# Gates' products where rounds of the recurrence meet, the start's transposes behind its products, a seventh place for the experts' weights

## The chip, the core and the metric

One NeuronCore of a Trainium2 chip runs the whole layer. Its engines work side by side, each through its own list of instructions: TensorE (PE, with its weight loads PEld), VectorE (DVE), ScalarE (ACT), GpSimd (POOL), and SyncE (SP), which issues the transfers between device memory and the core's memory. The metric is the time of one execution in microseconds on the device. Of TensorE the profile also shows the clock that was granted, as a share of 2.4 GHz.

## The reference, cut to what matters

```python
mod_x = silu(c) @ ada_w + ada_b               # 2048 -> 6 x 2048, for the tokens and the context
hx = rmsnorm(x) * (1 + sc1) + sh1             # hc likewise; 256 tokens each
px, pc = hx @ w_in, hc @ w_in                 # 2048 columns in; RWKV, attention, 4096 gate columns
yc_r, s_f, s_b = rwkv_branch(shift(pc), 0, 0)       # 16 heads of 64, forward and backward scan
yx_r, _, _     = rwkv_branch(shift(px), s_f, s_b)   # S = S*w - (S kk)(kk a)^T + v k^T ; y = S r
yx_d = diff_out(diff_attn_latent(q, k_all, v_all))
mix = (sigmoid(g0) * (yx_r @ w_pa) + sigmoid(g1) * (yx_d @ w_pb)) @ w_out
x = x + gt1 * mix
h2 = rmsnorm(x) * (1 + sc2) + sh2
x = x + gt2 * moe(h2)     # 32 experts 2048 -> 512 -> 2048, top 2 of one of 4 groups
# an expert: (silu(h w1) * (h w3)) w2
```

All in float32, 256 tokens and 256 of context.

## The kernel before, in words

The program goes in stages. `startup` loads the tokens and the context (`xt`) and scales their rows; `ada_first` multiplies the conditioning vectors by the first columns of ada_w, in four quarters (512 columns of the shift, 512 of the scale and so on), each from eight tiles of weights of 512 KB. A tile comes either from the `raw` places of the start (RAW0, L37, five of them) or from a piece of `xt`, once `tokens` (transposes, L693) has turned `xt` into columns and put its eight pieces on the list `free`. `modulate` (L704 to L724) then applies scale and shift and splits the result into a high and a low half for the products.

Behind the start runs one long background stream: the products of w_in, of ada's rest and of the gates, one tile of 256 KB after another. Each tile of weights is split in two: `whi` by ScalarE (L966), `wlo` by VectorE (L967), or by GpSimd while `self.low` says so. Each tile gives twelve products of 256 columns into `acc` (L490).

In the foreground stands the RWKV recurrence in four rounds, q = 0 to 3, four heads each. A round first computes features (`feats`: decay, `kq` L1091, the bonus `bon` and its product `pcf` L1104), then `within` and `braid` (products inside a chunk, `pa`), then `deltas`. That begins with the substitution `inverse`: 31 steps of a triangular inverse on VectorE (L1428, L1430), a transpose `ZT` (L1433), and TensorE's products `ph` (L1448) and `pz` (L1461). The rest of `deltas` is products (pW, pu, pS, py), with the features of the next round between them. Where a round's last products and the next round's features stand side by side, the rounds meet; the first meeting is that of q = 0 and q = 1. A generator of the foreground yields numbers; they are credits in microseconds, times 0.444, for which the background stream's steps are called in between. `inverse` yields 0.25 + 0.002 n n per step and `deltas` passes it on (times 1.0 for q < 3). That is the order of the program text; the scheduler of the framework then lists each engine's instructions by its own priorities and may move background work up.

The last stage is the experts, 16 pairs. A pair has 12 chunks of weights of 2 MB (four of w1, four of w3, four of w2), loaded by `weights` (L1755) from SyncE. The first eight go to eight places (`first`: four of tag w, xr, xd, ohl, and acc's); all later ones turn round over six (`slots`: w four times, xr, xd). A load waits for the last product that reads what its place held. A pair on TensorE: the products `pa` with w1 and w3 (L1834), the transposes of the gates and of the hidden rows (L1775, L1787), the `gather` of the next pair's tokens (L1766, four groups, each followed by VectorE's sum L1768), the products `po` with w2 (L1868; `down`), and their spread back to tokens (L1885; `back`, added on VectorE L1889, L1892), always one block behind. TensorE's order in this stage is the order of the program text. The last pair adds into `xr` and stores. Behind it stands the largest count of tokens of an expert (`most`, L1917 to L1922), loaded into a register: over 64, a second path would redo the experts, which is not taken here.

Of the kernel before, what the change touches and what calls it, by code (L numbers as in the profile page):

```python
# [10 lines left out]
F32R = mybir.dt.float32r  # L11
# [7 lines left out]
P = 128  # L19
D = 2048  # L20
KT = 16
# [15 lines left out]
RAW0, LOOK0 = 5, 8  # L37
# [140 lines left out]
def host_inputs(a):  # L178
# [10 lines left out]
    h["exp_w2"] = np.ascontiguousarray(np.asarray(a["exp_w2"])[0].reshape(E // 2, 2, 4, P, 4, 512).transpose(0, 4, 3, 1, 2, 5))  # L189
    h["ws"] = pack_parts(a)  # L190
# [6 lines left out]
def f32(ap):  # L197
    return ap.bitcast(F32)


class Body:
# [437 lines left out]
    def ada_first(self, c, w):  # L639
# [3 lines left out]
        for s in range(2):  # L643
            bank = []

            def fn(raw, k0, s=s, bank=bank):
                if k0 == 0:
                    bank.append(self.ps.tile([P, 512], F32, tag="ps", name="ada")[:, 0:w])
                for k in range(k0, k0 + n):
                    j = slice(k % 4 * 32, k % 4 * 32 + 32)  # L650
                    self.nc.tensor.matmul(bank[0][j, :], self.cs[:, k, :], raw[:, k - k0, :], start=(k < 4), stop=(k >= KT - 4),  # L651
                                          tile_position=(0, j.start))
                yield 0.5
                if k0 + n == KT:
                    if s == 0 and c == 0:
                        self.tokens()
                    self.modulate(c // P, w // P, s, bank[0])
# [29 lines left out]
    def tokens(self):  # L687

        nc = self.nc
        for k in range(KT):  # L690
            pt = self.psa.tile([P, 512], F32, tag="acc", name="pt")
            for i in range(4):
                nc.tensor.transpose(pt[:, i * P:(i + 1) * P], self.xt[:, i, k * P:(k + 1) * P], self.ident)  # L693
# [500 lines left out]
    def deltas(self, st, q):  # L1194
# [166 lines left out]
        yield 0.0  # L1361
# [343 lines left out]
    def moe(self, es):  # L1705
# [15 lines left out]
        slots = ["w"] * WB + ["xr", "xd"]  # L1721
        first = slots + ["ohl", wx]
# [24 lines left out]
        def weights(src, e=None):  # L1747
# [11 lines left out]
            return c  # L1759

# [57 lines left out]
        held = []  # L1818
        for pi in range(E // 2):
# [5 lines left out]
            for nm in ("exp_w1", "exp_w3"):  # L1825
# [13 lines left out]
                if last and nm == "exp_w1":  # L1839
                    gt2 = gate2()  # L1840
# [18 lines left out]
            oh, ol = ohl[:, 0], ohl[:, 1]  # L1859

            def down(w, hs, n):

                wd = hs.stop - hs.start
                o = pst("o", 4)[:, 0:wd]
                for f in range(4):
                    for e in range(2):
                        es_ = slice(e * 64, e * 64 + 64)
                        nc.tensor.matmul(o[es_, :], hT[:, f, es_], w[:, e, f, hs], start=(f == 0), stop=(f == 3),  # L1868
                                         tile_position=(0, e * 64))
                if last:  # L1870
                    g = tl("t", [P, 512], 2, tag="hm")[:, 0:wd]
                    nc.vector.scalar_tensor_tensor(g, o, gc, gt2[:, n * 512 + hs.start:n * 512 + hs.stop], ALU.mult, ALU.mult)
                    self.split(g, oh[:, n, hs], ol[:, n, hs])
                else:
                    nc.scalar.activation(oh[:, n, hs], o, AF.Copy, scale=gc)  # L1875
                    nc.vector.scalar_tensor_tensor(ol[:, n, hs], o, gc, f32(oh[:, n, hs]), ALU.mult, ALU.subtract)
                return oh[:, n, hs], ol[:, n, hs], slice(n * 512 + hs.start, n * 512 + hs.stop)
# [37 lines left out]
        pc = pst("t")  # L1915
        for i in range(2):
            nc.tensor.matmul(pc[:, 0:E], K["ones"], S0[:, i, :], start=(i == 0), stop=(i == 1))  # L1917
        most = tl("most", [P, 1])
        nc.vector.tensor_reduce(most, pc[:, 0:E], AX.X, ALU.max)
        mosti = tl("mosti", [P, 1], dt=I32)  # L1920
        nc.vector.tensor_copy(mosti, most)
# [66 lines left out]
```

## Time and profile before

| what | value |
| --- | --- |
| time, median of 3 runs | 2439.36 us (2437.42 to 2444.34) |
| profiled execution, its own time | 2450.88 us |
| its span | 2449.2 us |
| TensorE busy | 2297.4 us, 94% |
| VectorE busy | 1216.8 us, 50% |
| ScalarE busy | 779.1 us, 32% |
| GpSimd busy | 197.1 us, 8% |
| moved by the transfers | 691.46 MB, mean 282 GB/s |

The busy share is a mean over the stages above: the start up to about 60 us, the mixers up to about 1450, the experts from about 1500 on. A matmul row's time is from the start of the first to the end of the last of a run of like instructions, and float32 products appear as two records each. Busy TensorE is not TensorE at its peak, and whether a wait matters depends on the stage.

### The profile page before, as it was taken

The page shows a single profiled execution, that of the slowest core. Times are in us where ns is not written, and L with a number is a line of the kernel's source. Part 1 is how long each engine was busy: PE and PEld are TensorE (multiplying, and loading weights), DVE is VectorE, ACT ScalarE, POOL GpSimd, SP SyncE. Part 2 cuts the span into 40 slices and gives each one's busy share as a digit, 9 for nine tenths or more (in the row PEclk, how much of TensorE's full clock was granted, in tenths as well). Part 3 has the DMA queues.
Part 4 walks back from the last instruction along what each step waited for, and adds up shares of the span by engine and source line. Part 5 has one row for each costly group of instructions (what it writes and reads, how often), then busy time and mean ns, then how long its engine had stood idle before and what let it go on. Part 6 is the DMA issues. An engine that isn't in the chain of part 4 may idle for free.

```text
span 2449.2 us, 45035 instructions
## 1 busy us (share of the span) xinstructions
PE 2297.4 (94%) x18411; PEld 1612.3 (66%) x18411; DVE 1216.8 (50%) x2268; ACT 779.1 (32%) x1455; POOL 197.1 (8%) x260
## 2 busy tenths in 40 slices
PE   6999989899999999999998998999999999999997
PEld 2789977788998787787898985444433433433342
DVE  3355677868658577586865664222222222222223
ACT  3322336555436565566643441000000000000000
POOL 0110011202114233100000000000000000000000
PEclk9999999999999899899999999999999999999999
DMA  8977864657674243363447886899999999999997
GB/s 337 340 241 228 259 218 133 186 174 229 225 228 141 75 123 118 107 190 99 157 156 239 287 314 253 351 428 427 427 428 426 428 428 428 428 427 427 428 427 327
DMA packets 205476, 691.46 MB, mean 282 GB/s; under 512 B 31768, under 2 KB 69328, under 8 KB 179792
## 3 DMA queue, kind: packets, MB, share of 16 engines
q1 hardware_dynamic: 205264, 688.53, 75.2%
q8 instruction: 146, 2.39, 0.4%
q14 instruction: 66, 0.54, 0.1%
HBM read 666.66 MB, written 21.78 MB: 281 GB/s over the span
## 4 chain that ended last, share of the span: by engine, by line
PE 64%; DMA 18%; DVE 9%; issue 4%; ACT 3%; POOL 1%; SPq 0%; DVEq 0%; ACTq 0%; POOLq 0%
PE acc L490 13%; DMA xd<-in_exp_w_dram 10%; PE pa L1834 9%; PE po L1868 9%; PE acc L521 7%; PE pt L1766 5%; PE acc L815 4%; PE pt L1885 3%; DMA raw<-in_ws_dram 2%; DMA w<-in_exp_w_dram 2%; DVE prod L1428 2%; PE pc L1129 1%; PE ada L651 1%; DVE z L1430 1%; DMA g<-gate 1%
## 5 line engine op out<-in xcount | busy, mean ns | idle before, releaser
L966 ACT CAST whi<-raw 128x512 fp32r<-128x512 f32 (+1 forms) x463 | 280.4, 615 | 334.5 <-PE acc L490 150.7
L967 DVE TENSOR_TENSOR wlo<-raw,whi 128x512 fp32r<-128x512 f32 (+1 forms) x415 | 282.4, 693 | 82.6 <-ACT whi L966 80.6
L490 PE MATMUL acc<-xd,whi 128*128 128x256 f32 (+1 forms) x1248 | 267.1, 291 | 1.2 <-ACT whi L966 0.8
L490 PE MATMUL acc<-xr,whi 128*128 128x256 f32 (+1 forms) x1248 | 264.7, 290 | 1.3 <-ACT whi L966 0.8
L1834 PE MATMUL pa<-w,hg 128*64 128x512 f32 x1024 | 226.6, 594 | 15.8 <-DMA w<-in_exp_w_dram 12.5
L1868 PE MATMUL po<-w,hT 128*64 128x512 f32 (+1 forms) x1040 | 230.8, 590 | 1.6 <-DMA w<-in_exp_w_dram 0.8
L490 PEld LDWEIGHTS acc<-xd,whi 128*128 128x128 f32 (+1 forms) x1248 | 205.9, 191 | 19.6 <-issue 14.5
L490 PEld LDWEIGHTS acc<-xr,whi 128*128 128x128 f32 (+1 forms) x1248 | 205.5, 191 | 17.2 <-issue 12.8
L1781 DVE TENSOR_TENSOR hm<-hm,pa 128x512 f32<-128x512 f32 x16 | 11.0, 688 | 405.8 <-PE pa L1834 405.8
L490 PE MATMUL acc<-xr,wlo 128*128 128x256 f32 (+1 forms) x624 | 181.3, 291 | 4.2 <-DVE wlo L967 3.4
L490 PE MATMUL acc<-xd,wlo 128*128 128x256 f32 (+1 forms) x624 | 180.8, 290 | 2.6 <-DVE wlo L967 2.1
L1834 PEld LDWEIGHTS pa<-w,hg 128*64 128x64 f32 x1024 | 71.7, 137 | 165.5 <-issue 132.8
L607 DVE SCALAR_TENSOR_TENSOR ada<-raw,cs,ada 128x512 f32<-128x512 f32 x180 | 135.0, 758 | 90.4 <-DMA raw<-in_ws_dram 90.0
L1868 PEld LDWEIGHTS po<-w,hT 128*64 128x64 f32 x1040 | 70.4, 137 | 133.9 <-issue 127.3
L1892 DVE TENSOR_TENSOR acc<-acc,pt 128x512 f32<-128x512 f32 x112 | 75.3, 683 | 152.4 <-PE pt L1885 152.4
L1875 ACT ACTIVATE ohl<-po,gc 128x512 fp32r<-128x512 f32 x60 | 41.3, 689 | 296.6 <-PE po L1868 296.6
L1766 PE MATMUL pt<-pe,xa 128*128 128x128 f32 x1024 | 123.6, 279 | 5.9 <-DVE hg L1768 5.2
L1834 PE MATMUL pa<-xd,hg 128*64 128x512 f32 x496 | 113.1, 598 | 16.1 <-DMA xd<-in_exp_w_dram 16.1
L1834 PE MATMUL pa<-xr,hg 128*64 128x512 f32 x496 | 113.1, 598 | 15.5 <-DMA xr<-in_exp_w_dram 15.5
L1766 PEld LDWEIGHTS pt<-pe,xa 128*128 128x128 f32 x1024 | 118.6, 194 | 12.1 <-DVE hg L1768 8.8
L490 PEld LDWEIGHTS acc<-xr,wlo 128*128 128x128 f32 (+1 forms) x624 | 119.5, 192 | 8.9 <-DVE wlo L967 4.7
L490 PEld LDWEIGHTS acc<-xd,wlo 128*128 128x128 f32 (+1 forms) x624 | 119.4, 191 | 6.9 <-DVE wlo L967 3.5
(390 smaller groups left out, 4135.2 us busy)
## 6 DMA issues: line engine op xcount, KB each, us to landing
w<-in_exp_w_dram SPq DMA_DIRECT2D x128, 2048.0 KB
raw<-in_ws_dram SPq DMA_DIRECT2D x703, 256.0 KB
xr<-in_exp_w_dram SPq DMA_DIRECT2D x31, 2048.0 KB
xd<-in_exp_w_dram SPq DMA_DIRECT2D x31, 2048.0 KB
xt<-in_ws_dram SPq DMA_DIRECT2D x39, 512.0 KB
raw<-in_ws_dram SPq DMA_DIRECT2D x25, 512.0 KB
g<-gate SPq DMA_DIRECT2D x48, 128.0 KB
kvr<-own SPq DMA_DIRECT2D x16, 256.0 KB
```

The costliest lines, as they stand in the source:

```text
L490: m = nc.tensor.matmul(acc[j][:M, n * T:n * T + T], a[:, k2, j * M:(j + 1) * M], (rl if i == 1 else rh)[k], start=(k == 0 and i == 0 and s ...
L521: m = nc.tensor.matmul(acc[b][:, n * 256:n * 256 + 256], (ll if i == 2 else lh)[k][:, ts], (lo if i == 1 else hi)[:, k2, :], start=(k == 0 ...
L607: nc.vector.scalar_tensor_tensor(a, raw, c, a, ALU.mult, ALU.add)
L815: nc.tensor.matmul(acc[i], a[:, i * P:(i + 1) * P], b[:, k - k0, :], start=(k == 0 and q == 0), stop=(k == KT - 1 and q == 2))
L966: self.nc.scalar.copy(hi, src)
L967: (eng or self.nc.vector).tensor_tensor(lo, src, f32(hi), ALU.subtract)
L1428: nc.vector.tensor_tensor(prod[:, :n, :n], z[:, s + 1:, s + 1:], na[:, s, s + 1:].unsqueeze(1).to_broadcast([P, n, n]), ALU.mult)
L1766: nc.tensor.matmul(p[:, k * P:(k + 1) * P], xa[:, i, (k4 + k) * P:(k4 + k + 1) * P], pe[:, i, :], start=(i == 0), stop=(i == 1))
L1834: nc.tensor.matmul(a[es_, :], hg[:, k4 + k, es_], w[:, e, k, :], start=(k4 + k == 0), stop=(k4 + k == KT - 1), tile_position=(0, e * 64))
L1868: nc.tensor.matmul(o[es_, :], hT[:, f, es_], w[:, e, f, hs], start=(f == 0), stop=(f == 3), tile_position=(0, e * 64))
L1885: nc.tensor.matmul(y, one[:, i * P:(i + 1) * P], o, start=(h == 0), stop=(h == 1))
L1892: nc.vector.tensor_tensor(acc[:, i, os], acc[:, i, os], y, ALU.add)
```

## The change

Seven edits. (1) RAW0 from 5 to 7. (2) The transposes of `tokens` come behind the last product of ada's first quarter on TensorE; nothing is waited for, since both are TensorE's. (3) Credits: `inverse` passes 0.85 of its weight for q < 3, and `deltas` yields 3.0 at its end for q < 3, where it yielded 0. (4) A place `wm` of 2 MB joins the turning ones, which are now seven; the place of `ohl` goes from the first loads, and `ohl` is two small tiles, one block each. (5) w2 is packed on the host in halves of 256 columns; the last chunk is loaded as two transfers of 1 MB. (6) The next pair's gather stands between the blocks of `down` and not ahead of them. (7) The largest count is computed in the last pair; the register's load stays at the end.

```diff
-RAW0, LOOK0 = 5, 8
+RAW0, LOOK0 = 7, 8
...
+    h["exp_w2"] = np.ascontiguousarray(h["exp_w2"].reshape(E // 2, 4, P, 2, 4, 2, 256).transpose(0, 1, 2, 5, 3, 4, 6))
...
-                        self.tokens()
+                        self.tokens(m)
...
-                nc.tensor.transpose(pt[:, i * P:(i + 1) * P], self.xt[:, i, k * P:(k + 1) * P], self.ident)
+                m = nc.tensor.transpose(pt[:, i * P:(i + 1) * P], self.xt[:, i, k * P:(k + 1) * P], self.ident)
+                self.after(m, last)
...
-            yield w * (1.0 if q < 3 else 0.731)
+            yield w * (0.85 if q < 3 else 0.731)
...
-        yield 0.0
+        yield 3.0 if q < 3 else 0.0
...
-        slots = ["w"] * WB + ["xr", "xd"]
-        first = slots + ["ohl", wx]
+        slots = ["w"] * WB + ["xr", "xd", "wm"]
+        first = slots + [wx]
...
+            if parts:
+                for v, x in zip(parts(c), src):
+                    nc.sync.dma_start(v, x)
+                return c
...
+        def halves(w):
+            return w.rearrange("p a b c -> p (a b c)").rearrange("p (h e f n) -> p h e f n", h=2, e=2, f=4)
...
+        def largest():
+            pc = pst("t")
+            for i in range(2):
+                nc.tensor.matmul(pc[:, 0:E], K["ones"], S0[:, i, :], start=(i == 0), stop=(i == 1))
+            nc.vector.tensor_reduce(most, pc[:, 0:E], AX.X, ALU.max)
+            nc.vector.tensor_copy(mosti, most)
...
                 if last and nm == "exp_w1":
+                    largest()
...
-            for k4 in range(4, KT, 4) if not last else ():
-                gather(pe, hg, k4)
-            ohl = tl("ohl", [P, 2, 4, 512], dt=F32R)
...
+                ohl = tl("ohl", [P, 2, 512], 2, dt=F32R)
...
-                        nc.tensor.matmul(o[es_, :], hT[:, f, es_], w[:, e, f, hs], start=(f == 0), stop=(f == 3),
-                                         tile_position=(0, e * 64))
+                        v = halves(w)[:, hs.start // 256:hs.stop // 256, e, f, :]
+                        nc.tensor.matmul(o[es_, :].rearrange("p (h n) -> p h n", n=256), hT[:, f, es_], v, start=(f == 0),
+                                         stop=(f == 3), tile_position=(0, e * 64))
...
-                    o = down(weights(I["exp_w2"][pi, n]), slice(0, 512), n)
+                    o = down(down_weights(n), slice(0, 512), n)
                     if prior:
                         back(*prior)
                     prior = o
+                    if n < 3:
+                        gather(pe, hg, 4 * n + 4)
...
-                ws = [weights(I["exp_w2"][pi, n]) for n in range(4)]
+                ws = [down_weights(n) for n in range(3)]
+                ws.append(weights([I["exp_w2"][pi, 3, :, h] for h in range(2)], parts=lambda c: [halves(c)[:, h] for h in range(2)]))
```

On TensorE the program began with the transposes of `xt` (L693) mixed with ada's products (L651), both of the start. Before:

```order
L693 MATMUL pt<-cst_58,xt 128x128 x15
L651 MATMUL ada<-raw,cs 32x512 x2
L693 MATMUL pt<-cst_58,xt 128x128 x3
L651 MATMUL ada<-raw,cs 32x512 x2
L693 MATMUL pt<-cst_58,xt 128x128 x3
L651 MATMUL ada<-raw,cs 32x512 x2
L693 MATMUL pt<-cst_58,xt 128x128 x6
L651 MATMUL ada<-raw,cs 32x512 x2
L693 MATMUL pt<-cst_58,xt 128x128 x13
L651 MATMUL ada<-raw,cs 32x512 x2
```

After, where the same lines are L695 and L653, and L710 is the transpose of `row`:

```order
L653 MATMUL ada<-raw,cs 32x512 x16
L695 MATMUL pt<-cst_58,xt 128x128 x64
L710 MATMUL pt<-cst_58,row 128x128 x4
L653 MATMUL ada<-raw,cs 32x512 x12
L653 MATMUL ada<-xt,cs 32x512 x4
L710 MATMUL pt<-cst_58,row 128x128 x4
L653 MATMUL ada<-xt,cs 32x512 x8
```

All of the first quarter's products now stand ahead of the transposes, and the second quarter takes `raw` for longer before it comes to `xt`.

On GpSimd, at the second meeting (features of q = 2, with `wlo` the low half of a gate's weights, `bon` and `ce` pieces of the features, `z` the next substitution's start). Before:

```order
L1083 TENSOR_TENSOR bon<-bon,f 128x256
L967 TENSOR_TENSOR wlo<-raw,whi 128x512 x2
L1097 COPY ce<-cx 128x8
L1070 MEMSET cx 128x8
L967 TENSOR_TENSOR wlo<-raw,whi 128x512
L1081 COPY bon<-f 128x256
L967 TENSOR_TENSOR wlo<-raw,whi 128x512 x2
L1097 COPY ce<-cx 128x8
L1070 MEMSET cx 128x8
L619 MEMSET ev 128x256
L1083 TENSOR_TENSOR bon<-bon,f 128x256
L1424 MEMSET z 128x1024
```

After:

```order
L1086 TENSOR_TENSOR bon<-bon,f 128x256
L970 TENSOR_TENSOR wlo<-raw,whi 128x512
L621 MEMSET ev 128x256
L1100 COPY ce<-cx 128x8
L1073 MEMSET cx 128x8
L1084 COPY bon<-f 128x256
L1100 COPY ce<-cx 128x8
L1073 MEMSET cx 128x8
L1086 TENSOR_TENSOR bon<-bon,f 128x256
L1427 MEMSET z 128x1024
```

Of the five low halves ahead of the substitution one is left; the others are VectorE's.

On TensorE in the first pairs of experts (`pa` products with w1 and w3, `pt` from `pe` the gather, `po` products with w2, `pt` from `ohl` the spread back). Before:

```order
L1834 MATMUL pa<-acc,hg 64x512 x8
L1775 MATMUL pt<-cst_58,pg 128x128 x2
L1766 MATMUL pt<-pe,xa 128x128 x8
L1787 MATMUL pt<-cst_58,hm 128x128 x4
L1766 MATMUL pt<-pe,xa 128x128 x24
L1868 MATMUL po<-w,hT 64x512 x16
L1885 MATMUL pt<-ohl,one 128x512 x4
L1868 MATMUL po<-w,hT 64x512 x8
L1885 MATMUL pt<-ohl,one 128x512 x4
L1868 MATMUL po<-w,hT 64x512 x8
L1885 MATMUL pt<-ohl,one 128x512 x4
L1834 MATMUL pa<-xr,hg 64x512 x8
```

After:

```order
L1859 MATMUL pa<-acc,hg 64x512 x8
L1789 MATMUL pt<-cst_58,pg 128x128 x2
L1780 MATMUL pt<-pe,xa 128x128 x8
L1801 MATMUL pt<-cst_58,hm 128x128 x4
L1893 MATMUL po<-w,hT 64x512 x8
L1780 MATMUL pt<-pe,xa 128x128 x8
L1893 MATMUL po<-w,hT 64x512 x8
L1910 MATMUL pt<-ohl,one 128x512 x4
L1780 MATMUL pt<-pe,xa 128x128 x8
L1893 MATMUL po<-w,hT 64x512 x8
L1910 MATMUL pt<-ohl,one 128x512 x4
L1780 MATMUL pt<-pe,xa 128x128 x8
```

The products with w2 start behind the first group of the gather, and a group of the gather stands behind each of the first three.

## Rows read from the trace of the kernel before

**Rows 1.** The page's slices of the span: share of busy transfers, in tenths.

```profile
DMA  8977864657674243363447886899999999999997
```

**Rows 2.** Timeline of the start: start us, us, engine, line, [idle before <-releaser].

```profile
13.83 1.54 PE L693 MATMUL pt<-cst,xt 128*128 128x128 f32 x6 [13.83 <-DVE xt L684]
...
19.61 1.92 PE L651 MATMUL ada<-raw,cs 128*32 128x512 f32 x4
...
27.29 1.64 PE L693 MATMUL pt<-cst,xt 128*128 128x128 f32 x13
...
41.46 1.05 PE L651 MATMUL ada<-xt,cs 128*32 128x512 f32 x4 [1.39 <-DMA xt<-in_ws_dram]
...
45.30 1.05 PE L651 MATMUL ada<-xt,cs 128*32 128x512 f32 x4 [0.23 <-DMA xt<-in_ws_dram]
...
34.71 5.82 SPq L411 DMA_DIRECT2D xt<-in_ws_dram  x8
```

**Rows 3.** Windows: PE, PEld, DVE, ACT, POOL busy (x), granted clock, DMA share, GB/s.

```profile
20.00:40.00 20.00, 19.31 (x101) 7.43 (x97) 7.01 (x11) 5.18 (x9) 0.00 (x0) 1.00 0.75 245
```

**Rows 4.** Timeline of TensorE: first substitution's products, first meeting.

```profile
789.90 2.31 PE L1448 MATMUL ph<-ZT,A 32*32 32x32 f32 x128 [1.07 <-DVE ZT L1433]
...
868.46 0.70 PE L1104 MATMUL pcf<-bon,cst 128*128 128x256 f32 x2 [1.99 <-DVE bon L1101]
```

**Rows 5.** Windows in the recurrence, same columns.

```profile
790.00:810.00 20.00, 20.00 (x401) 17.88 (x401) 7.74 (x10) 6.36 (x10) 1.35 (x2) 0.57 0.21 67
869.00:882.00 13.00, 13.00 (x125) 12.63 (x124) 5.28 (x10) 6.35 (x12) 0.52 (x1) 0.61 0.31 99
1010.00:1014.00 4.00, 1.68 (x9) 0.84 (x6) 3.73 (x6) 3.02 (x7) 1.11 (x1) 0.97 0.82 221
1014.00:1027.00 13.00, 13.00 (x106) 12.23 (x107) 6.66 (x12) 2.96 (x5) 0.00 (x0) 0.50 0.40 131
1161.00:1183.00 22.00, 21.98 (x258) 18.36 (x251) 15.24 (x27) 13.66 (x27) 1.11 (x2) 1.00 0.37 121
```

**Rows 6.** Timeline of GpSimd and VectorE in the second and third meeting.

```profile
999.96 3.41 POOL L967 TENSOR_TENSOR wlo<-raw,whi 128x512 fp32r<-128x512 f32 x2
...
1000.46 1.78 DVE L1091 SCALAR_TENSOR_TENSOR kq<-a,ic 128x512 f32<-128x512 f32 x1
...
1159.74 0.68 DVE L1091 SCALAR_TENSOR_TENSOR kq<-a,ic 128x512 f32<-128x512 f32 x1
```

**Rows 7.** Timeline of TensorE and SyncE's queue in the first pair of experts.

```profile
1531.93 3.60 PE L1834 MATMUL pa<-ohl,hg 128*64 128x512 f32 x16
...
1541.90 5.62 PE L1766 MATMUL pt<-pe,xa 128*128 128x128 f32 x48 [0.34 <-DVE hg L1768]
1547.45 7.09 PE L1868 MATMUL po<-w,hT 128*64 128x512 f32 x32
...
1532.14 0.33 SPq L1755 DMA_DIRECT2D xd<-in_exp_w_dram  x1
...
1551.15 13.18 SPq L1755 DMA_DIRECT2D w<-in_exp_w_dram  x4
```

**Rows 8.** Windows in the experts, same columns.

```profile
1540.00:1550.00 10.00, 9.65 (x74) 7.67 (x75) 4.98 (x14) 0.59 (x1) 0.00 (x0) 1.00 0.16 67
1550.00:1560.00 10.00, 10.00 (x46) 3.70 (x42) 2.75 (x5) 2.07 (x3) 0.00 (x0) 1.00 0.78 305
1700.00:2400.00 700.00, 655.77 (x3298) 280.25 (x3296) 167.60 (x321) 46.65 (x71) 0.00 (x0) 1.00 1.01 428
```

**Rows 9.** Timeline of TensorE and VectorE at the end.

```profile
2433.12 1.20 PE L1885 MATMUL pt<-ohl,one 128*128 128x512 f32 x4
2434.42 1.95 PE L1868 MATMUL po<-w,hT 128*64 128x256 f32 x16
...
2441.41 0.75 DVE L1889 TENSOR_TENSOR xr<-xr,pt 128x256 f32<-128x256 f32 x2 [0.48 <-PE pt L1885]
...
2442.78 0.15 DVE L1921 CAST mosti<-most 128x1 int32<-128x1 f32 x1
```

More of the change, by code (lines that the diff above doesn't have):

```diff
@@ L650, in fn @@
                     j = slice(k % 4 * 32, k % 4 * 32 + 32)
-                    self.nc.tensor.matmul(bank[0][j, :], self.cs[:, k, :], raw[:, k - k0, :], start=(k < 4), stop=(k >= KT - 4),
-                                          tile_position=(0, j.start))
+                    m = self.nc.tensor.matmul(bank[0][j, :], self.cs[:, k, :], raw[:, k - k0, :], start=(k < 4),
+                                              stop=(k >= KT - 4), tile_position=(0, j.start))
                 yield 0.5
@@ L685, in startup, with tokens @@
         self.ms = sp.tile([P, 2, KT, 2], F32, name="ms")
-    def tokens(self):
+    def tokens(self, last):
         nc = self.nc
@@ L1745, in moe, with weights @@
         chunks, prev = [0], [None]
-        def weights(src, e=None):
+        def weights(src, e=None, parts=None):
             n = chunks[0]
@@ L1759, in weights, with down_weights @@
             return c
+        def halves(w):
+            return w.rearrange("p a b c -> p (a b c)").rearrange("p (h e f n) -> p h e f n", h=2, e=2, f=4)
+        def down_weights(n):
+            return weights(I["exp_w2"][pi, n].rearrange("p h e f n -> p (h e f n)").rearrange("p (a b c) -> p a b c", a=2, b=4))
         def gather(pe, hg, k4):
@@ L1818, in moe @@
         held = []
+        def largest():
[4 more added lines that the diff above has]
+            nc.vector.tensor_copy(mosti, most)
+        most = tl("most", [P, 1])
+        mosti = tl("mosti", [P, 1], dt=I32)
         for pi in range(E // 2):
@@ L1855, in moe @@
             hT = turned(hm)
-            for k4 in range(4, KT, 4) if not last else ():
-                gather(pe, hg, k4)
-            ohl = tl("ohl", [P, 2, 4, 512], dt=F32R)
-            oh, ol = ohl[:, 0], ohl[:, 1]
             def down(w, hs, n):
                 wd = hs.stop - hs.start
+                ohl = tl("ohl", [P, 2, 512], 2, dt=F32R)
+                oh, ol = ohl[:, 0, 0:wd], ohl[:, 1, 0:wd]
                 o = pst("o", 4)[:, 0:wd]
@@ L1872, in down @@
                     nc.vector.scalar_tensor_tensor(g, o, gc, gt2[:, n * 512 + hs.start:n * 512 + hs.stop], ALU.mult, ALU.mult)
-                    self.split(g, oh[:, n, hs], ol[:, n, hs])
+                    self.split(g, oh, ol)
                 else:
-                    nc.scalar.activation(oh[:, n, hs], o, AF.Copy, scale=gc)
-                    nc.vector.scalar_tensor_tensor(ol[:, n, hs], o, gc, f32(oh[:, n, hs]), ALU.mult, ALU.subtract)
-                return oh[:, n, hs], ol[:, n, hs], slice(n * 512 + hs.start, n * 512 + hs.stop)
+                    nc.scalar.activation(oh, o, AF.Copy, scale=gc)
+                    nc.vector.scalar_tensor_tensor(ol, o, gc, f32(oh), ALU.mult, ALU.subtract)
+                return oh, ol, slice(n * 512 + hs.start, n * 512 + hs.stop)
             def back(hi, lo, os, one=one, pi=pi, last=last):
@@ L1912, in moe @@
         order.close()
[L1915 to L1921, printed above, removed]
         most = nc.values_load(mosti[0:1, 0:1], min_val=0, max_val=T)
@@ L1956, in moe @@
                             o = pst("o", 4)
-                            c = weights(I["exp_w2"][bass.ds(pi, 1), n, :, e].rearrange("o p f n -> p (o f) n"), e)
+                            c = weights([I["exp_w2"][bass.ds(pi, 1), n, :, :, e].rearrange("o p h f n -> p (o h) f n")],
+                                        parts=lambda c: [halves(c)[:, :, e]])
                             for f in range(4):
-                                nc.tensor.matmul(o, hT[:, f, :], c[:, e, f, :], start=(f == 0), stop=(f == 3))
-                            ob = tl("ob", [P, 512], tag="ohl")
+                                nc.tensor.matmul(o.rearrange("p (h n) -> p h n", n=256), hT[:, f, :], halves(c)[:, :, e, f, :],
+                                                 start=(f == 0), stop=(f == 3))
+                            ob = tl("ob", [P, 512], 2, tag="ohl")
                             nc.scalar.copy(ob, o)
```

## The prediction

> **What bounds the kernel now.** I read the page's slices first. TensorE is the busiest engine, and the transfers have two faces: in the last third the DMA row stands at nine tenths and more, before that mostly between two and eight [rows 1]. So the kernel is two programs: until about 1530 us TensorE sets the end, and stretches in which it waits or runs at the lower clock are what can be won; in the experts the stream of weights does. From 1700 to 2400 us TensorE is busy 655.77 of 700 us while the transfers run at 428 GB/s without a pause [rows 8]: a chunk of 2.097 MB every 4.9 us. There a faster TensorE buys nothing, an earlier stream everything. Then I read the four places the change touches: the chain of TensorE's and SyncE's rows at the start, TensorE's waits and granted clock in the recurrence, the first pair of experts, and the last ten microseconds.
>
> All sums are against the profiled execution, 2450.88 us (span 2449.2). The median of the runs shown is 2439.36, 11.5 lower; I take the sum off 2450.88 and then subtract 11.5.
>
> **The start (two more raw places, products ahead of the transposes).** Before, five raw places leave the transfers at 245 GB/s from 20 to 40 us [rows 3]; the 64 transposes stand between the products of the first quarter, and the eight loads into places that the transposes free are issued only at 34.71. The last four products of the second quarter wait for those, the first 1.39 us, and the last ends at 45.30 + 1.05 = 46.35; they follow the landings, (45.30 - 41.46) / 3 = 1.28 apart [rows 2]. After, the first quarter's eight groups of four records come first, from about 14 us. Four at 1.92 and four at 1.05 (the first and the later rows of the same product) are 11.9 us, to 25.9; the landings, 14 + 7 x 1.28 = 23, are no later. The transposes take 64 records at 1.64 / 13 = 0.126 [rows 2], 8.1 us, to 34.0; the row's transposes 0.7; eight more products at 1.05, 8.4 us, to 43.1. By the order fourteen of these sixteen groups now come from raw places, each of the seven used twice, and only the last two from places that the transposes free at 34.0. With the 6.75 us that the eight loads of before took to the first landing (34.71 to 41.46) they are there at 40.8; their products are due at 43.1 - 2 x 1.05 = 41.0. Gain 46.35 - 43.1 = **3.2 us**. Ends: all eight first products at 1.92 give 46.6, a loss of 0.3; products bound by the landings alone give 14 + 8 x 1.28 + 8.1 + 0.7 + 8.4 = 41.4, a gain of 4.9. I take 3.2 since both durations stand in the trace side by side.
>
> The same product takes 1.92 us at 19.61 and 1.05 at 41.46 [rows 2], though the granted clock reads 1.00 from 20 us on [rows 3]. The Trainium skill's page "TensorE: Matmul & The Clock Gate", section "What's actually happening", has it that the array starts throttled and that activity lifts it. By that rule the first products of the new order, which stand where the transposes stood, run slow and the sum is the 3.2 above; by the clock column alone they would take 1.05 and it would be the 4.9. The trace's durations side with the page.
>
> **The recurrence (0.85 instead of 1.0 per step of the substitution, 3.0 at the end of a round).** The weights only set how many products of the gates are called for; the scheduler then moves them up, so I go by the order of the instructions. Low-clock stretches follow a wait of TensorE each time: 1.07 us ahead of the first substitution's products (L1448), then 0.57 over 790 to 810; 1.99 us ahead of the first meeting's (L1104) [rows 4], then 0.61 over 869 to 882; 4.00 - 1.68 = 2.3 us idle in the second meeting, then 0.50 (the 1.2 GHz level) over 1014 to 1027. The third meeting has neither wait nor low clock: 21.98 of 22 us busy at 1.00 [rows 5]. What differs in the second is the feature chain: GpSimd computes two lo halves, 3.41 us, and beside it VectorE's kq takes 1.78 us against 0.68 in the third meeting [rows 6]. In the new order GpSimd has no lo half between the second feature passes' copies there, and TensorE has 58 products of the gates behind the last product on a (pa) instead of 49. Nine more records are about 9 x 13.00 / 106 = 1.1 us of cover [rows 5], and the chain is shorter by kq's 1.1 us and as much again in whatever else ran beside GpSimd: together about the wait of 2.3. So I forecast that this wait and the low stretch behind it go: 2.3 + 13.00 x 0.50 = **8.8 us**. Ends: nothing, if the wait stays above what lowers the clock, and 8.8. The first meeting keeps GpSimd's lo halves and has 57 products instead of 63; I leave it as it is, and the first substitution too, with three products more in front of it than before (4572 to 4569, counted from the start). From a meeting to the substitution's products there are 226, 289 and 296 products of the gates after, 214, 281 and 288 before; the 50 that stood behind the last product of the fourth round are inside its substitution now. The work is the same, and TensorE does it in any place: nothing.
>
> The clock falls behind waits of 1.07, 1.99 and 2.3 us [rows 4, 5]. The same page and section of the Trainium skill call the moment of the change "run-variable". By that, the 6.5 us of low clock (13.00 x 0.50) are there in some executions only, the gain is 2.3 in the others, and the sum would be 6.5 less: 2427.5. One profile cannot tell, and the number above stands on the one there is.
>
> **The experts (a seventh steady place, gather between the products with w2).** Before, the chunk loaded at 1532.14 is the last for which a place is free; the next loads are issued at 1551.15, when the first product with w2, behind all of the next pair's gather (48 records, 5.62 us, from 1541.90), has ended [rows 7]. In 1540 to 1550 only 0.67 MB move, 1.57 us of the full rate; in 1550 to 1560 3.05 MB, 7.1 us [rows 8]: the stream is dry from 1541.6 to 1552.9, 11.3 us, and flows 1.75 us behind its issue. After, the place of the third w3 chunk is one of the seven steady ones: free at 1531.93 + 3.60 = 1535.5, its load keeps the stream going to 1541.6 + 4.9 = 1546.5. The first product with w2 starts where the gather stood, 1541.9, and takes 7.09 / 2 = 3.55; then a gather of 5.62 / 3 = 1.87 [rows 7], a product, back's 1.20 [rows 9], a gather, and so on: places come free at 1545.5, 1550.9, 1557.5 and 1564.1, and the stream is dry 0.7 + 0.5 + 1.75 + 1.7 = 4.7 us. Three waits like the 0.34 that the gather shows [rows 7] make it 5.7. Gain 11.3 - 5.7 = **5.6 us**; it carries to the end, because the stream never pauses after. Ends: 0, if the stream catches up nothing, for instance as the later chunks wait instead; 11.3, if it never dries.
>
> w2 is read in runs of 256 columns by TensorE and loaded in the same bytes. TensorE has 44 us of slack in 700 [rows 8]; a product may get 6% slower before it shows. Nothing; as a bound, 64 products with w2 by 0.1 us are 6.4 us over the stage, under that slack.
>
> **The end.** The largest count now stands in the last pair. VectorE's last adds end at 2441.41 + 0.75 = 2442.16, the cast of the count at 2442.93 [rows 9]: **0.8 us**. The 6.3 us from there to the end of the span stay, since the register's load and the branch stay behind it: the bounds are 0.8 and 7.1. The last chunk in two halves lets the first two 256-column groups start earlier, but TensorE is busy up to the last four (2434.42, behind 2433.12 + 1.20 = 2434.32 [rows 9]): nothing.
>
> **Sum.** -3.2 - 8.8 - 5.6 - 0.8 = -18.4: 2432.5 for an execution like the profiled one, 2421.0 against the median.
>
> **Rivals.** *The meeting does not gain.* The second meeting's wait stays over 1 us, or another place loses as much: the chain of features has the same instructions, and one product of 0.12 us here or there decides little. -9.6, 2429.8. For it: the credits move by one or two products at most places. Against: the third meeting, without lo halves on GpSimd, has no wait.
> *More low stretches go.* The first substitution has three products more ahead of it; if its wait shrinks below what lowers the clock, 20.00 x 0.43 + 1.07 = 9.7 go as well, 2411.3; if the first meeting's goes too, 13.00 x 0.39 + 1.99 = 7.1 more, 2404.2. Against: 57 products for 63 at the first meeting.
> *Half of it.* The start keeps its waits on transfers (-1.2), the stream's gain is halved (-3.0), the end 0.8: -5.0, 2434.4.
> *Slower.* With 15% less called for inside the substitution, TensorE runs dry ahead of the third and fourth substitutions' products: a wait of over 1.07 us there costs what it costs in the first, 9.7 us each, and the third meeting, good now, could take the second's 8.8: +28.2 - 18.4 = +9.8, 2449.2; without the second meeting's gain 2458. It decides where products run out 1 us or more before VectorE has ZT (L1433). For it: the cut is made there. Against: the order has more products ahead of these, not fewer.
>
> **How the numbers follow.** Forecast 0.42, meeting without gain 0.26, more stretches gone 0.16, half 0.08, slower 0.08. What a measurement can tell from no change is 0.3%, 7.3 us: below 2432.0 counts as faster. The forecast and the third case lie there, and two thirds of the second (0.17): with a little of the rest 0.77; slower 0.08; the rest, 0.15, the same. The range goes from the low end of the third case to just past the half case: 2404 to 2436; the forecast's own is 2413 to 2428.
>
> **What would show it.** Right: transposes in one piece from about 26 us and the second quarter's last product before 44; no GpSimd lo half and no wait over 1 us in the second meeting, with a clock of 1.00 behind it; a load at about 1535 us of the old time scale and less than 6 us without transfers around the first w2 products; nothing of VectorE behind the last add. Wrong: a low clock that has only moved to another place of the recurrence, a stream that is dry 10 us again between the first and second pair, or waits on the DMA between the first quarter's products at the start.

## The result, and the profile after

The changed kernel takes 2413.97 us (median of 4, 2410.8 to 2414.49) against 2441.85 (4, 2437.42 to 2446.05): ratio 0.9882, 95% interval 0.9856 to 0.9907, 27.9 us faster. The forecast was 2421.0, 18.4 off the kernel before. The profiled execution took 2410.8 us, 40.1 less than the profiled one of before, which was 9 above its median.

Timeline of the changed kernel's start, TensorE and SyncE's queue, columns as in [rows 2]:

```profile
17.84 6.16 PE L653 MATMUL ada<-raw,cs 128*32 128x512 f32 x20 [17.84 <-DMA raw<-in_ws_dram]
...
27.66 7.21 PE L695 MATMUL pt<-cst,xt 128*128 128x128 f32 x64
...
35.23 2.78 PE L653 MATMUL ada<-raw,cs 128*32 128x512 f32 x24
37.83 1.30 PE L653 MATMUL ada<-xt,cs 128*32 128x512 f32 x8
...
45.81 0.38 PE L523 MATMUL acc<-whi,xd 128*128 128x256 f32 x1 [0.45 <-ACT whi L969]
...
31.12 6.75 SPq L413 DMA_DIRECT2D xt<-in_ws_dram  x8
```

The second quarter ends at 39.1 us, where [rows 2] had 46.35, and the first product of w_in starts at 45.81; before, it starts at 53.02:

```profile
53.02 0.39 PE L521 MATMUL acc<-whi,xd 128*128 128x256 f32 x1 [1.55 <-ACT whi L966]
```

Windows of the start of w_in's products, of before and then of after (columns as in [rows 3]):

```profile
53.00:63.00 10.00, 8.30 (x44) 8.09 (x45) 4.10 (x9) 1.74 (x3) 0.61 (x1) 0.66 1.03 407
```

```profile
46.00:56.00 10.00, 8.27 (x68) 6.49 (x68) 3.93 (x8) 1.83 (x4) 0.45 (x1) 1.00 1.03 408
```

Before, the first 10 us of these products run at a mean clock of 0.66, after at 1.00. That is 3 us more: from w_in's first product to the attention's first it is 291.7 us before and 288.7 after.

Windows of after: first substitution's products (20 us), first and second meeting from pc (the product that follows pcf) to pm (the mean product of L1375, now L1378), second substitution's products. They answer to [rows 5]:

```profile
777.14:797.14 20.00, 20.00 (x527) 17.29 (x528) 10.55 (x15) 10.67 (x17) 2.66 (x3) 1.00 0.29 87
847.89:858.15 10.26, 10.18 (x146) 9.31 (x146) 6.80 (x12) 6.25 (x12) 2.25 (x3) 1.00 0.54 177
987.31:997.48 10.17, 10.17 (x149) 9.32 (x147) 7.36 (x15) 6.78 (x14) 1.11 (x2) 1.00 0.57 175
912.91:932.91 20.00, 20.00 (x476) 16.92 (x478) 9.29 (x12) 9.21 (x15) 2.11 (x2) 0.83 0.20 65
```

And of before, for the same pieces:

```profile
789.90:809.90 20.00, 20.00 (x401) 17.97 (x402) 7.84 (x10) 6.26 (x10) 1.45 (x2) 0.57 0.21 68
868.38:883.28 14.90, 14.82 (x147) 14.14 (x147) 5.90 (x12) 6.44 (x12) 1.11 (x2) 0.66 0.31 101
1014.20:1030.14 15.94, 15.94 (x146) 14.94 (x145) 6.52 (x12) 4.65 (x8) 1.11 (x2) 0.59 0.33 106
936.56:956.56 20.00, 20.00 (x474) 17.46 (x475) 9.87 (x14) 9.24 (x15) 3.29 (x3) 0.83 0.31 102
```

The same 146 records of a meeting take 10.2 us at full clock and 15 to 16 at 0.59 to 0.66. Three of these four low stretches are gone; the second substitution's is still there.

First pair of experts, windows of after, answering to [rows 8]:

```profile
1505.00:1515.00 10.00, 9.33 (x60) 5.50 (x60) 4.09 (x10) 1.27 (x2) 0.00 (x0) 1.00 0.95 385
1515.00:1525.00 10.00, 9.68 (x50) 4.70 (x46) 2.77 (x5) 1.37 (x2) 0.00 (x0) 1.00 0.85 341
1525.00:1535.00 10.00, 9.68 (x52) 4.58 (x52) 5.35 (x11) 0.69 (x1) 0.00 (x0) 1.00 0.84 301
1535.00:1545.00 10.00, 10.00 (x48) 3.54 (x46) 1.29 (x2) 0.00 (x0) 0.00 (x0) 1.00 0.99 377
```

Against 428 GB/s that is 1.0 + 2.0 + 3.0 + 1.2 = 7.2 us without transfers, 11.3 before. The new place's load is issued where the forecast had it: the experts start 34.4 us earlier than before, so 1501.20 is 1535.6 on the old time scale, and the next load 1545.9:

```profile
1501.20 0.33 SPq L1762 DMA_DIRECT2D wm<-in_exp_w_dram  x1
1511.56 20.07 SPq L1762 DMA_DIRECT2D w<-in_exp_w_dram  x4
```

The end, after; the last add ends at 2403.24, 5.9 us ahead of the end of the span (7.0 before), and no cast of the count follows it:

```profile
2402.49 0.75 DVE L1914 TENSOR_TENSOR xr<-xr,pt 128x256 f32<-128x256 f32 x2 [0.48 <-PE pt L1910]
```

The stages, from the starts of marked instructions in each profile (us). "Start": to the attention's first product (L1590). "Round": from ph to pm. "pm to ph": first round's pm to the second's ph. "M1, M2, M3": clock from pc to pm at the meetings. "Experts": first product to the end of the last with w1 and w3. "End": from there.

| profile | start | round 1 (clock after ph) | pm to ph | round 2 (clock after ph) | round 3 | round 4 | M1, M2, M3 | experts | end |
| --- | --- | --- | --- | --- | --- | --- | --- | --- | --- |
| before | 344.8 | 93.4 (0.57) | 53.3 | 93.6 (0.83) | 80.0 | 43.5 | 0.66 0.59 1.00 | 915.8 | 31.1 |
| after | 334.5 | 81.0 (1.00) | 54.8 | 84.6 (0.83) | 82.3 | 40.5 | 1.00 1.00 1.00 | 911.8 | 29.3 |
| e1 start | 334.9 | 93.4 (0.57) | 53.3 | 93.3 (0.83) | 79.9 | 43.5 | 0.66 0.58 1.00 | 915.8 | 31.3 |
| e2 credits | 344.1 | 83.7 (0.83) | 55.2 | 90.3 (0.51) | 82.2 | 40.5 | 1.00 1.00 1.00 | 918.2 | 31.6 |
| e3 experts | 344.0 | 93.4 (0.57) | 53.3 | 95.6 (0.83) | 79.9 | 43.6 | 0.66 0.54 1.00 | 911.4 | 29.3 |
| e4 no credits | 334.8 | 93.4 (0.57) | 53.3 | 93.3 (0.83) | 79.9 | 43.9 | 0.66 0.58 1.00 | 915.8 | 29.4 |
| e5 after again | 334.6 | 81.7 (1.00) | 55.0 | 91.1 (0.51) | 82.3 | 41.8 | 1.00 1.00 1.00 | 913.2 | 29.3 |
| e6 0.85 | 345.3 | 88.9 (0.83) | 54.4 | 89.1 (0.80) | 80.5 | 50.0 | 0.66 0.58 1.00 | 916.1 | 31.1 |
| e7 3.0 | 342.1 | 83.6 (1.00) | 55.6 | 87.7 (0.77) | 87.8 | 40.5 | 1.00 1.00 0.58 | 918.3 | 31.1 |
| e8 raw | 339.1 | 89.0 (0.83) | 53.3 | 93.3 (0.83) | 79.9 | 43.5 | 0.66 0.59 1.00 | 917.8 | 31.7 |
| e9 fill | 332.1 | 88.1 (0.57) | 57.6 | 81.1 (1.00) | 79.5 | 43.7 | 1.00 1.00 1.00 | 913.3 | 29.5 |
| e10 gather ahead | 332.8 | 81.1 (1.00) | 55.0 | 85.5 (0.83) | 82.2 | 40.7 | 1.00 1.00 1.00 | 910.8 | 29.8 |
| e11 six places | 334.9 | 83.7 (0.83) | 55.1 | 84.7 (0.78) | 82.5 | 40.9 | 1.00 1.00 1.00 | 916.8 | 29.2 |
| e12 fill, ahead | 336.3 | 83.7 (0.83) | 57.1 | 81.2 (0.98) | 80.1 | 43.6 | 1.00 1.00 1.00 | 912.8 | 29.4 |

### The profile page after: what moved, and what is told of

It reads as the page before. It is cut to its first block, busy times and chain, and to the rows that moved or that the text cites. A ratio compares the mean times of both kernels' runs of the same rounds, so it can differ in the third digit from the quotient of the medians.

```text
span 2409.1 us, 45078 instructions
## 1 busy us (share of the span) xinstructions
PE 2271.1 (94%) x18411; PEld 1590.6 (66%) x18411; DVE 1213.6 (50%) x2274; ACT 779.6 (32%) x1455; POOL 187.3 (8%) x254
## 4 chain that ended last, share of the span: by engine, by line
## 5 line engine op out<-in xcount | busy, mean ns | idle before, releaser
L970 DVE TENSOR_TENSOR wlo<-raw,whi 128x512 fp32r<-128x512 f32 (+1 forms) x419 | 287.2, 699 | 85.2 <-ACT whi L969 82.5
L1859 PE MATMUL pa<-w,hg 128*64 128x512 f32 x1152 | 256.1, 595 | 14.6 <-DMA w<-in_exp_w_dram 11.5
L1859 PEld LDWEIGHTS pa<-w,hg 128*64 128x64 f32 x1152 | 80.0, 137 | 177.0 <-issue 150.8
L609 DVE SCALAR_TENSOR_TENSOR ada<-raw,cs,ada 128x512 f32<-128x512 f32 x180 | 134.8, 760 | 85.5 <-DMA raw<-in_ws_dram 85.4
L1893 PE MATMUL po<-w,hT 128*64 128x512 f32 (+1 forms) x624 | 139.1, 588 | 6.2 <-ACT hT L1803 6.1
L1780 PE MATMUL pt<-pe,xa 128*128 128x128 f32 x1024 | 131.5, 283 | 10.1 <-DVE acc L1917 8.8
L1794 ACT ACTIVATE hm<-pa 128x512 f32<-128x512 f32 x16 | 9.6, 597 | 270.0 <-PE pa L1859 270.0
L492 PE MATMUL acc<-ch,whi 128*128 128x256 f32 (+1 forms) x320 | 96.6, 302 | 0.0
L1803 ACT COPY hT<-pt 128x512 f32<-128x512 f32 x16 | 9.4, 585 | 266.7 <-PE pt L1801 266.7
```

Of the source, the lines that this page charges most:

```text
L492: m = nc.tensor.matmul(acc[j][:M, n * T:n * T + T], a[:, k2, j * M:(j + 1) * M], (rl if i == 1 else rh)[k], start=(k == 0 and i == 0 and s ...
L609: nc.vector.scalar_tensor_tensor(a, raw, c, a, ALU.mult, ALU.add)
L970: (eng or self.nc.vector).tensor_tensor(lo, src, f32(hi), ALU.subtract)
L1780: nc.tensor.matmul(p[:, k * P:(k + 1) * P], xa[:, i, (k4 + k) * P:(k4 + k + 1) * P], pe[:, i, :], start=(i == 0), stop=(i == 1))
L1794: nc.scalar.activation(hm, a1, AF.Silu)
L1803: nc.scalar.copy(hT, pt.rearrange("p (f s) -> p f s", f=4))
```

## The experiments

Ratios are to the kernel before, run beside it on the same chip, with 95% intervals. There the times of before spread more than in the first comparison: beside e1 to e4, 32 executions from 2431 to 2464, median 2448.4.

**e1, the start alone.**

```diff
-RAW0, LOOK0 = 5, 8
+RAW0, LOOK0 = 7, 8
...
+                self.after(m, last)          # in tokens
```

> The kernel before with the start's two edits alone (seven raw places, transposes behind the first quarter's products). TensorE's order behind the start is that of before. Prediction's step: 3.2 us faster. The trace of after read as it stands: its first product of w_in begins at 45.81 us against 53.02, so 7.2 us faster, and the second quarter ends at about 39 us. Rival 'chance': low-clock stretches of the recurrence come and go from one execution to the next with the same order, so that this profile has others than before (790 to 810, 869 to 882, 1014 to 1027 us), although nothing there is changed; the time over five rounds is then still 3 to 7 us faster.

Ratio 0.9968 (0.9939 to 0.9996), 7.5 us faster. The profile has the start 9.9 shorter and every stage behind it as before to 0.3 us, low clock included: the start is worth some 10 us by the profile, three times the forecast. The low stretches of before stand again in this profile, so the rival does not show here; e5 and the last section come back to it.

**e2, the credits alone.**

```diff
-            yield w * (1.0 if q < 3 else 0.731)
+            yield w * (0.85 if q < 3 else 0.731)
...
-        yield 0.0
+        yield 3.0 if q < 3 else 0.0
```

> The kernel before with the credits alone (0.85 and 3.0). Prediction's step: 8.8 us faster, the second meeting without wait and at full clock, the first meeting and the first substitution as before. The trace of after read as it stands: first substitution to its round's end 81.0 us against 93.4, second 84.6 against 93.5, third 2.3 longer, fourth 2.9 shorter: some 17 to 20 us faster. Rival 'chance': the low stretches of before are those of one execution; then the medians move only by the waits that go, 1.99 at the first meeting and 2.3 at the second, 2 to 5 us.

0.9934 (0.9908 to 0.996), 14.1 faster: more than the forecast, a little less than the trace of after. Both meetings run at full clock. The rival's 2 to 5 us lie below the interval, which begins at 9.8.

**e3, the experts alone** (the changed kernel with the start's and credits' edits undone; against the code of before, shortened:

```diff
+        slots = ["w"] * WB + ["xr", "xd", "wm"]
+        first = slots + [wx]
...
+                    largest()
...
+                    if n < 3:
+                        gather(pe, hg, 4 * n + 4)
```

with w2 in halves).

> The kernel before with the experts' edits alone (seventh place, gather between the products with w2, w2 in halves, largest count early). Prediction's steps: 5.6 + 0.8 = 6.4 us faster. The trace of after: from the first product of the experts to the end 941.2 us against 946.9, so 5.7 faster. Rival 'stream': the time is set by the transfers and these catch up anyway, 1 us or less from the end alone.

0.9976 (0.9951 to 1.0001), 6.3 faster, and by the profile 4.4 + 1.8 = 6.2: the forecast's 6.4. The interval just reaches no change, so it is the profile that shows this gain and not the time.

**e4, the changed kernel with the old credits.**

```diff
-            yield w * (0.85 if q < 3 else 0.731)
+            yield w * (1.0 if q < 3 else 0.731)
...
-        yield 3.0 if q < 3 else 0.0
+        yield 0.0
```

> The changed kernel with the old credits (1.0 and 0.0): start and experts alone. Prediction's steps: 3.2 + 6.4 = 9.6 us faster than before. The trace of after: 7.2 + 5.7 = 13 faster. Rival 'chance': over 20 us faster, most of the 27.9 that the whole change measured, since the credits are worth 5 at most.

0.996 (0.9936 to 0.9984), 8.3 faster. The rival falls: without the credits most of the gain is missing. The experts' 915.8 look like no gain, but in this profile their first 10 us run at 0.76, in before and after at 1.00. In e2 and e7, with the old stage and 0.76 and 0.77 there, they take 918.2 and 918.3.

**e5, the changed kernel again**, nothing edited.

> The changed kernel itself once more, beside the same runs of before as the next three. If the gains are fixed by the order of instructions: 24 to 32 us faster, and in its profile the first substitution to its round's end again near 81.0 us (93.4 in four of four executions with the old credits), the second near 84.6. If the clock falls or not by chance behind the same wait of 1.06 us: somewhere between 81 and 93 there, and 16 to 24 us faster.

0.9896 (0.9866 to 0.9926), 22.0 faster: in the range that the expectation gave to chance, with an interval that reaches into both. The first round repeats, at 81.7; the second is 91.1, 6.5 longer than in the first profile of the same kernel, 5.9 of it between the substitution's products and the second meeting, where the clock differs (windows of e5: first substitution, second substitution):

```profile
778.83:798.83 20.00, 19.32 (x511) 16.55 (x512) 10.01 (x14) 9.97 (x16) 2.69 (x3) 1.00 0.29 85
...
915.61:935.61 20.00, 20.00 (x394) 18.55 (x395) 7.55 (x10) 6.07 (x9) 2.11 (x2) 0.51 0.20 65
```

**e6 and e7, one credit each.**

```diff
+            yield w * (0.85 if q < 3 else 0.731)                # e6 alone
...
+        yield 3.0 if q < 3 else 0.0                             # e7 alone
```

> The kernel before with 0.85 alone (no 3.0 at the rounds' ends). Its order has 58 products of the gates behind the last product on a at the first meeting (63 before, 57 with both credits) and 45 at the second (49, 58). Prediction's mechanism (cover at the second meeting decides): not faster than before, the second meeting waits 2 us or more, 0 to 5 us slower. Rival 'fewer in the substitution' (the first substitution and first meeting gain because less is called for inside): 5 to 14 us faster, first round 84 us or less instead of 93.4.

> The kernel before with 3.0 at the rounds' ends alone. Its order has 57 products behind the last product on a at the first meeting and 62 at the second, 34 more in front of the third substitution. Prediction's mechanism: the whole gain of the credits is here, 10 to 17 us faster, both meetings without a wait before pcf. Rival 'fewer in the substitution': 5 us or less.

e6: 1.0025 (0.9999 to 1.0051), 6.4 slower. e7: 0.9981 (0.996 to 1.0002), 4.0 faster. Both intervals just reach no change. Neither carries the 14. With 0.85 alone both meetings keep the low clock and the fourth round takes 50.0 us. With 3.0 alone the first two meetings are cured and the third falls (window of e7):

```profile
1144.39:1160.49 16.10, 16.10 (x147) 15.10 (x146) 6.29 (x11) 4.70 (x8) 1.11 (x2) 0.58 0.35 117
```

So e6 is not faster, as expected, and e7 is half right: its 4.0 is the rival's number, but 3.0 cures the first two meetings, and with 0.85 beside it (after, e2) the third does not pay for it.

The two runs also part the two reasons that the forecast gave for the second meeting. From its first to its second pcf e6 has the shorter chain (27.5 us, 31.3 before) and no lo half on GpSimd, but only 45 of the gates' products in front: TensorE waits 0.35 and 1.26 us, and the clock falls to 0.58. In e7 the chain takes 29.7 us with five lo halves, but 62 products stand in front: it waits 0.62 us, and the clock stays at 1.00. There the products in front go with the clock, the lo halves do not; that is one profile each. The rows of pcf, of e7's first and third meeting and then of e6's second:

```profile
857.76 0.70 PE L1104 MATMUL pcf<-bon,cst 128*128 128x256 f32 x2 [1.74 <-DVE bon L1101]
...
1144.07 1.09 PE L1104 MATMUL pcf<-bon,cst 128*128 128x256 f32 x2 [1.15 <-DVE bon L1101]
```

```profile
1005.94 1.20 PE L1104 MATMUL pcf<-bon,cst 128*128 128x256 f32 x2 [1.26 <-DVE bon L1101]
```

**e8, the raw places alone.**

```diff
-RAW0, LOOK0 = 5, 8
+RAW0, LOOK0 = 7, 8
```

> The kernel before with the two more raw places alone; TensorE's order at the start is that of before, with the transposes between the first quarter's products. The start's two edits together gained 9.9 us to the attention's first product (46.2 + 288.7 against 53.0 + 291.8). If the places do it (loads no longer wait for the transposes): 5 to 10 us by the trace. Rival 'order': the transposes between the products keep the first quarter late, and the places alone give 0 to 3.

0.9998 (0.9971 to 1.0025), no difference that was measured, though the profile has the start 5.7 shorter. The places give a good half of the start's 9.9 in the profile; the rest is the order.

**e9, products thrown away ahead of the second substitution's** (nothing reads their result).

```diff
+        if fill:
+            dm = pst("dm")
+            for _ in range(fill):            # 3 where q == 1
+                nc.tensor.matmul(dm, K["bones"], z.rearrange("b s t -> b (s t)")[:, 0:512], start=True, stop=True)
         ZT = H = tl("ZT", [P, NB, 32], tag="b3")
```

> The changed kernel with three products thrown away (128x512, on the last state of z, overwritten by nothing that is used) ahead of the second substitution's products L1451, where TensorE waits 3.0 to 3.5 us in all four profiles with the new credits and then runs at 0.51 to 0.83 over 20 us. The scheduler keeps the order up to there; behind it the second meeting has 61 products of the gates behind the last product on a (58), the third 44 (45). Theory 'the wait costs by the clock that falls behind it': wait in pieces under 1.5 us, the round from the second substitution to its end 80 to 83 us instead of 84.6 and 91.1, 26 to 32 us faster than before. Rival 'a wait costs its length': thrown-away work in idle time changes nothing, 84 to 91 us, 22 to 28 faster.

0.9859 (0.9817 to 0.9901), 31.6 faster; not to be told from the changed kernel's 0.9882 and 0.9896. Timeline and windows of e9:

```profile
918.85 4.51 PE L1438 MATMUL dm<-z,cst 128*128 128x512 f32 x6 [2.56 <-DVE z L1433]
923.29 2.21 PE L1455 MATMUL ph<-ZT,A 32*32 32x32 f32 x128
```

```profile
919.00:923.00 4.00, 4.00 (x6) 1.31 (x6) 3.96 (x3) 0.36 (x1) 1.53 (x2) 0.59 0.58 182
923.29:943.29 20.00, 20.00 (x536) 17.65 (x535) 9.00 (x15) 10.79 (x18) 1.27 (x1) 1.00 0.10 29
```

My expectation of a short wait was wrong: the products could start only with the last z, 2.56 us late, and the clock fell (0.59 over 919 to 923). But after 4.5 us of these 512-column products it was back, and the 20 us behind ran at 1.00, where the profiles with the new credits and the small products in that place have 0.51 to 0.83. They cost 2.7 us themselves (57.6 for 54.9) and the round gets 3.5 to 10 shorter than in the two profiles of the changed kernel. By the round's 81.1 the rival falls; the time alone would not show it.

**e10 and e11, the seventh place and the gather apart.**

```diff
+            for k4 in range(4, KT, 4) if not last else ():      # e10: ahead of down
+                gather(pe, hg, k4)
...
-                    if n < 3:
-                        gather(pe, hg, 4 * n + 4)
...
-        slots = ["w"] * WB + ["xr", "xd", "wm"]                 # e11
-        first = slots + [wx]
+        slots = ["w"] * WB + ["xr", "xd"]
+        first = slots + ["wm", wx]
```

> The changed kernel with the next pair's gather again all ahead of the products with w2: the seventh place alone. From the first product of the experts to the end of the last product with w1 and w3 the profiles show 915.8 to 918.3 us with the old stage and 911.4 to 915.8 with the new. By the prediction's model the stream is dry 6.4 us with the place alone (1546.5 to 1552.9 on the old time scale), so 4.9 of the 11.3 us are gained: 911 to 914. Rival 'the gather does it': 916 or more.

> The changed kernel with the seventh place used for one first load only, so that six turn as before; gather between the products with w2. By the prediction's model the stream is dry 5.6 + 0.5 + 1.75 + 1.7 = 9.6 us, so 1.7 of 11.3 are gained: 915 to 917 from the first product of the experts to the end of the last with w1 and w3. Rival 'the gather does it': 911 to 914, as with both.

0.9886 (0.9842 to 0.993) and 0.9912 (0.988 to 0.9944); these intervals overlap. By the profiles the place alone keeps the whole gain of the experts' stage (910.8), the gather alone none (916.8). The stream, windows of e10 and then of e11:

```profile
1510.00:1520.00 10.00, 10.00 (x57) 4.96 (x56) 3.03 (x7) 1.21 (x2) 0.00 (x0) 1.00 0.44 162
1520.00:1530.00 10.00, 10.00 (x45) 3.66 (x45) 4.32 (x7) 1.54 (x3) 0.00 (x0) 1.00 1.03 434
```

```profile
1510.00:1520.00 10.00, 9.32 (x60) 5.63 (x61) 4.37 (x10) 1.27 (x2) 0.00 (x0) 1.00 0.49 179
1520.00:1530.00 10.00, 9.68 (x51) 4.71 (x48) 2.64 (x4) 1.19 (x2) 0.00 (x0) 1.00 0.89 354
1530.00:1540.00 10.00, 9.68 (x51) 4.64 (x51) 5.47 (x11) 0.87 (x2) 0.00 (x0) 1.00 0.82 292
```

With the gather ahead the places come free one after another and the stream has one hole of 6.2 us; with the gather between them each release is late, 5.8 + 1.7 + 3.2 us in three holes.

**e12, e9 and e10 together.**

```diff
+        for n, w in enumerate(self.inverse([s["A"] for s in st], 3 if q in (1,) else 0)):
...
+            for k4 in range(4, KT, 4) if not last else ():
+                gather(pe, hg, k4)
```

> Both of the last round's edits on the changed kernel: three products thrown away ahead of the second substitution's, and the gather all ahead of the products with w2 (with the seventh place). If they add up and cost nothing: 26 to 36 us faster than before, second substitution to the round's end 80 to 83 us at full clock from L1451 on, and 910 to 914 us from the first product of the experts to the end of the last with w1 and w3. Rival 'no better than the changed kernel': 22 to 28 us faster. The first substitution (wait of 1.06 us) may again run at 0.57 or at 1.00, which alone is 8 us.

0.9892 (0.9863 to 0.9922), 25.3 faster: the second round at 81.2 and the experts at 912.8 as hoped, but the time is the rival's, no better than the changed kernel. No kernel here is shown to beat it.

## Why the prediction was right, and where its steps were not

The time lay in the range and the direction held; the sum was 9.5 us short of the measured 27.9 and 3.6 short of e5's 22.0. That it came so near is in part luck: by the two profiles, which lie 40.1 apart, three terms were too small by some 7, 7 and 6 us (the start, the first meeting, the first substitution), the last of these by what one execution happened to get; the profile of before is itself 9 us slow, and 1 to 9 us that were not in the sum go the other way.

**The start: 3.2 forecast, some 10 in the profiles.** The term failed in its price. I took 1.05 us for four records, which is the length of a group that stands alone; back to back 24 take 2.78, or 0.46 for four. [Rows 2] left out the row of before that points to it, 16 records in 2.88 us:

```profile
37.20 2.88 PE L651 MATMUL ada<-raw,cs 128*32 128x512 f32 x16
```

The eight first groups start 4 us later than I put them, with the first landing, but take 9.9 us for 11.9, the 64 transposes 7.2 for 8.1, and the second quarter 4 for 8.4. The other part, 3 us, was not in the sum at all: the low clock behind the waits ahead of w_in's first products, 0.66 there before. That early products run slow, which I weighed, is so: in after a record takes 1.06 us (median) up to 22.9 us and 0.61 from there to 28, while the clock column reads 1.00 in both. But the groups start 1.26 us apart in both, the pace of the landings (1.28 in my sum), so the slow records cost nothing; the 3.2 and the other reading's 4.9 rested on the same wrong price for the second quarter.

**The second meeting: 8.8 forecast, right.** From the first pcf of that meeting to pm it is 47.7 us in before and 38.6 to 39.2 in after, e2 and e5, at 1.00: 8.5 to 9.1 less. Of the two reasons that I gave, e6 and e7 bear out the products in front and not the lo halves.

**The first meeting "stays": wrong.** From its first pcf to pm it takes 45.4 us in all six profiles with the old order or 0.85 alone, 38.7 in after, e2 and e5. I compared 57 products with 63 and called it less cover, and didn't price the chain: VectorE's kq ends the features in 0.68 us in after, 1.75 before, and GpSimd has three lo halves from the second pass's copy of `bon` to pcf, 4.6 us, for five, 7.6 us:

```profile
866.25 1.75 DVE L1091 SCALAR_TENSOR_TENSOR kq<-a,ic 128x512 f32<-128x512 f32 x1
```

```profile
845.81 0.68 DVE L1094 SCALAR_TENSOR_TENSOR kq<-a,ic 128x512 f32<-128x512 f32 x1
```

The wait at pcf goes from 1.99 us to 0.64. What made it shorter is argued from these rows, not shown apart. Nor does its length alone decide the clock: in e7 TensorE still waits 1.74 us at this pcf (kq stays at 1.77) and the clock holds, while 1.15 us at the third meeting's pcf, in the same execution, are followed by 0.58; in e6 it waits 1.94 and the clock falls.

**The first substitution "stays": its wait did, its clock didn't.** The wait is 1.02 to 1.08 us in twelve of the fourteen profiles, 2.11 in e11 and 3.36 in e6. With the old credits four of five run at 0.57 behind it, with both new ones 1.00, 1.00, 1.00, 0.83, 0.83, 0.83 and 0.57 in seven. From ph to the first pcf that is 48.0 us before and 42.3 after: 5.6 of the first round's 12.4, and not fixed by the order (48.0 in four profiles, 43.6 in e8): in the first comparison the third case of the forecast, at a chance of 0.16, is in large part what happened, though its condition, a shorter wait, was not met here.

**What I left out.** The second substitution waits longer, 2.9 to 3.5 us in the profiles with both new credits and the small products there, for 2.0 to 2.7, and may fall to 0.51; pm to ph, which holds that wait, is 1.5 to 2.0 longer and the third round 2.3, while the fourth is 1.7 to 3.0 shorter. Together these give back some 1 us (after) to 9 us (e5) of what the meetings bring.

**The experts: 5.6 forecast, 4.0 by the first profile, the place right.** The dry time came to 7.2 us instead of 5.7. I gave part of it to the gather; e10 and e11 show that the seventh place does it alone. The bound on w2 took 64 products, where the stage has some 520 (1040 records), so it bounded nothing; but a record takes 592 ns (median) before and 593 after. The half case takes 3.0 for half of 5.6, where 2.8 is meant, and no row gives its 1.2 for the start. **The end:** 0.8 forecast, 1.1 to the last add.

**The rival "slower"** did not come: the third and fourth substitutions wait 0.00 to 0.26 us in every profile. Its other loss, the third meeting's, does come in e7, 16.1 us at 0.58, but there 3.0 stands alone and nothing less is called for inside the substitutions.

## What to carry to other kernels

Price a product by a run that stands back to back, and a wait by its length plus the clock behind it: at two meetings of before 2 us of waiting cost 7 to 9, though e7's 1.74 us cost 1.4. Look for what follows the wait too: behind three waits of before the clock read 0.57 to 0.66 over 15 to 20 us. A buffer more is worth a model of who frees which place when; the same model said which of two edits would do the work.

## What the runs showed that was not expected

One kernel's executions differ by the clock they get: over 32 executions of before, time and mean granted clock go together (correlation -0.96, 2.2 us for each 0.001), while the lengths of most stages repeat to 0.3 us between profiles with the same order there. Part of what differs is whether a low stretch follows a wait of 1.0 to 3.5 us in the substitutions: the two profiles of the changed kernel are 15.5 us apart, 6.5 of them in the second round. Another part is the experts' first 10 us: 0.76 to 0.81 in e2, e4, e7, e8 and e12, 1.00 in the other nine profiles. That 4.5 us of 512-column products behind 2.56 us of waiting are followed by the full clock is seen in e9 and again in e12 (4.1 us behind 2.48, then 0.98 over 20 us); with the small products in their place five profiles have 0.51 to 0.83. Why the same wait of 1.06 us leads to 0.57 in one execution and to 1.00 in another, and why 1.74 us hold in e7 where 1.15 do not, stays open.
